# Modulation vectors: the four column tiles of the matmul array take columns of a block, and one transposition gives shift or scale

## The chip, the core and the metric

The program runs on one core of a Trainium2 chip. The metric is the device time of one execution in microseconds (us), as a median over runs. A core has TensorE for matmuls (PE, with its weight loads shown apart as PEld), VectorE (DVE), ScalarE (ACT), GpSimd (POOL) and SyncE (SP, which here mostly issues DMAs). SBUF is the on-chip memory that the engines read, PSUM the accumulator memory that TensorE writes.

## The reference

Two layers of a diffusion backbone run over 256 latent tokens and 256 context tokens of width 1024. Each layer first makes its modulation (adaLN) from two condition vectors, `c` for the latents and `c_ctx` for the context:

```python
for i in range(DEPTH):                                   # DEPTH = 2, D_MODEL = 1024
    mod_l = silu(c)     @ w_mod[i] + b_mod[i]            # 1024 -> 6144
    mod_c = silu(c_ctx) @ w_mod[i] + b_mod[i]
    sh1, sc1, g1, sh2, sc2, g2       = split(mod_l, 6)
    csh1, csc1, cg1, csh2, csc2, cg2 = split(mod_c, 6)
    zl = split_cols((layernorm0(x)     * (1 + sc1)  + sh1)  @ w_in[i])
    zc = split_cols((layernorm0(h_ctx) * (1 + csc1) + csh1) @ w_in[i])
    ...                                                  # four token mixers, merge gates, w_out
    x = layernorm(alpha * x + g1 * y_l)
    x = layernorm(alpha * x + g2 * conv_ffn(layernorm0(x) * (1 + sc2) + sh2))
    ...                                                  # the same for h_ctx with csh2, csc2, cg1, cg2
```

A modulation is thus a matrix with two rows (one for each condition) times `w_mod`, with 1024 rows and 6144 columns a layer. It is a small part of the arithmetic and a large part of the weights: 50 MB of f32 for both layers. Shift and scale are wanted with the 1024 features on the partitions (as per-partition scalars), the gates g1 and g2 as rows.

## The kernel before

**Weights.** All weights stand in one tensor of tiles `in_wt`, 128 x 1024 f32 (512 KB) each, in the order in which the program uses them. SP issues their DMAs into buffers `wraw`. For the large products a tile is split on ACT (`wH`, the value rounded to fp32r) and on DVE or POOL (`wL`, the rest), and products are summed of high and low parts (`gft`, `gtf`, `up`: input projections and the ConvFFN). A tile of `w_mod` is used as it is, in fp32, and needs no split.

**Modulation.** `w_mod` falls into 24 blocks of 512 columns (12 a layer: `nb` 0 to 11, kind `nb // 2` = shift1, scale1, gate1, shift2, scale2, gate2), each of four tiles, so 96 tiles. `mod_jobs` (from L781) makes four jobs of a block. A job waits for its tile and issues four matmuls of 128 x 32 weights (`cz`, the two conditions in 32 columns, one chunk of 128 of the 1024 rows) by 128 x 256 moving columns. They stand in the four column tiles of the array, 32 columns each, so they run side by side: column tile k takes another chunk of rows, and the result `modp`, 128 partitions x 512, holds four partial sums for each condition. Behind the fourth tile ACT copies `modp` to `modrow` (128 x 512). What follows depends on the kind:

- Shift or scale (16 blocks): four matmuls `modcp` take a 128 x 128 piece of `modrow` as the weights and the constant `sel` (128 x 2, ones at every 32nd partition) as the moving operand. That sums the four partial sums and puts the features on partitions. DVE adds bias into `modc`, which the modulation of the tokens (`modulate`, tiles `xmt`, `xmH`, `xms`, `xm`, `xmL`) reads.
- Gate (8 blocks): one matmul `modr` takes `sel` as the weights and `modrow` as the moving operand. DVE adds the bias (`modbm`), and a DMA puts the row into DRAM for later.

**Where the tiles stand.** The first 16 tiles (blocks 0, 2, 1, 3 of layer 0) are the start of the program: nothing else can go before them. Their accumulators come from the pool of the projections (`pgt`, three banks), those of all later blocks from `pq`, which has one. 52 tiles (13 blocks: nine of shift or scale, four of gates) are fill: they are put one by one between the projections of layer 0's mixers. 28 tiles (table LATE, blocks of layer 1) stand at the ends of stages: before layer 0's ConvFFN, between the layers, and before layer 1's ConvFFN.

**What sets the order.** The program is written out by a planner (`Net`, from L118). It keeps an estimated clock for every engine, adds the estimated duration of each instruction to it, and takes what could start first (`pump` L297): the next step of the weight stream (`pick` L353, `feed` L368, `splitter` L386), or one of the threads of the mixers, which carry chains of small steps (names `gd_`, `ret_`, `hg_`, `lru_`, `ro_`). An engine runs its instructions in the order that comes out. So an instruction with another shape also moves others, on all engines.

Of the kernel before, what the change touches and what calls it, by code (L numbers as in the profile page):

```python
# [9 lines left out]
F32 = mybir.dt.float32  # L10
# [4 lines left out]
ALU = mybir.AluOpType  # L15
# [102 lines left out]
class Net:  # L118
# [440 lines left out]
    def load_consts(self):  # L559
        const, I, V, A, S = self.const, self.I, self.V, self.A, self.S  # L560

        c0 = const.tile([128, 8, 2], F32, name="c0")
        S.dma_start(c0, I["cc"])
        self.sel_c = const.tile([128, 2], F32, name="sel")
        S.dma_start(self.sel_c, I["c_sel"])
        th = const.tile([128, 8, 2], F32, name="cth")
        A.activation(th, c0, AF.Tanh, scale=0.5)
        V.scalar_tensor_tensor(th, in0=th, scalar=1.0, in1=c0, op0=ALU.add, op1=ALU.mult)
        self.cz = const.tile([128, 8, 32], F32, name="cz")
        V.memset(self.cz, 0.0)  # L570
        V.tensor_scalar(self.cz[:, :, 0:2], th, 0.5, None, op0=ALU.mult)
        ck = self.ck = const.tile([128, 6, 128], F32, name="ck")
        self.ident, self.UI, self.LI, self.US, self.LS, self.perm = (ck[:, j, :] for j in range(6))
        self.par = [const.tile([128, NP], F32, name=f"par{i}") for i in range(DEPTH)]
        for i in range(DEPTH):
            S.dma_start(self.par[i], I["par"][i])
        self.msk = const.tile([128, 1664], U8, name="msk")
        self.hgm = self.msk[:, 0:1024].rearrange("p (l t) -> p l t", l=8)
        self.gdm = self.msk[:, 1024:1536].rearrange("p (l d t) -> p l d t", l=2, d=2)
        self.umask = self.msk[:, 1536:1664]  # L580
        self.ones = const.tile([128, 128], F32, name="ones")
        V.memset(self.ones, 1.0)
        self.modc = [const.tile([128, 4, 8, 2], F32, name=f"modc{i}") for i in range(DEPTH)]
        self.rowd = [self.dr.tile([2, 2, 1024], F32, name=f"rowd{i}") for i in range(DEPTH)]
# [196 lines left out]
    def mod_jobs(self, i, nb, early=False):  # L781

        mm = self.PE.matmul
        st = {}

        def mk(kk):
            def run():
                if kk == 0:
                    if early:
                        st["row"] = self.tile(self.fw, [128, 512], F32, "f_row", "modrow", 4)  # L790
                        st["ps"], st["rec"] = self.pgt([128, 512], "modp")
                    else:
                        if self.mod_th is not None:
                            self.finish(self.mod_th)
                        st["row"] = None
                        st["ps"], st["rec"] = self.tile(self.pq, [128, 512], F32, "modp", "modp", 1), []
                W, ps = self.next_tile()[0], st["ps"]
                half, kh = kk % 2, kk // 2

                for k in range(4):  # L800
                    mm(ps[32 * k:32 * k + 32, half * 256:half * 256 + 256], self.cz[:, kh * 4 + k, :], W[:, k * 256:(k + 1) * 256],
                       start=(kk == 0), stop=(kk == 3))
                if kk == 3:
                    self.evac(st["rec"], ps, evac)
                    self.mod_th = st["rec"][0]
                yield

            def evac(ps):
                row = st["row"] if early else self.ev([128, 512], "modrow")
                self.A.activation(row, ps, AF.Copy)  # L810
                kind = nb // 2
                if kind in (2, 5):
                    half, c0 = kind // 3, (nb % 2) * 512
                    yield "PE", [row], "free"
                    pr = self.pmt([128, 512], "modr")
                    mm(pr[0:2, :], self.sel_c, row, start=True, stop=True)
                    bm = self.ev([2, 512], "modbm")
                    self.S.dma_start(bm, self.I["bm"][i, nb:nb + 1, :].partition_broadcast(2))
                    yield "DVE", [bm, pr]

                    self.V.tensor_tensor(bm, bm, pr[0:2, :], op=ALU.add)
                    self.V.tensor_scalar(bm, bm, 0.5, None, op0=ALU.mult)
                    self.S.dma_start(self.rowd[i][half, :, c0:c0 + 512], bm)
                    return
                yield "PE", [row], "free"
                kind = {0: 0, 1: 1, 3: 2, 4: 3}[kind]
                pc = self.pmt([128, 4, 2], "modcp")
                for j in range(4):
                    mm(pc[:, j, :], row[:, j * 128:(j + 1) * 128], self.sel_c, start=True, stop=True)
                j0 = (nb % 2) * 4  # L830
                b0 = _P["bm"][0] + kind * 8 + j0
                self.V.scalar_tensor_tensor(self.modc[i][:, kind, j0:j0 + 4, :], in0=pc, scalar=float(kind % 2),
                                            in1=self.par[i][:, b0:b0 + 4].unsqueeze(2).broadcast_to([128, 4, 2]), op0=ALU.add, op1=ALU.add)
            j = _Job([(("w_mod", i, nb * 512 + (kk % 2) * 256, 4, 256, (kk // 2) * 4), 1024)], run)
            j.mode = "plain"
            j.early = early
            j.cost = MOD_EVERY
            return j
        return [mk(kk) for kk in range(4)]


# [1346 lines left out]
def _constants():  # L2188
    c = {}
# [18 lines left out]
    hgm[:, 0, :] = u == t  # L2208

    c["c_msk"] = np.ascontiguousarray(np.concatenate([z.reshape(128, -1).astype(np.uint8) for z in (hgm, gdm, u < t)], axis=1)).view(np.float32)  # L2210
    sel = np.zeros((128, 2), np.float32)
    for j in range(2):
        sel[j::32, j] = 1.0
    c["c_sel"] = sel
    pos = np.arange(256)
    inv = (np.float32(10000.0) ** (-np.arange(16, dtype=np.float32) / np.float32(16))).astype(np.float32)
    rope = np.zeros((128, 2, 256), np.float32)
# [30 lines left out]
def _host_arrays(a, specs):  # L2248
# [13 lines left out]
    for i in range(DEPTH):  # L2262
# [19 lines left out]
        for d in range(2):  # L2282
            for ty, nm in enumerate(("lru_w_a", "lru_w_i")):
# [3 lines left out]
    out["bm"] = a["b_mod"].reshape(DEPTH, 12, 512)  # L2287
    out.update(par=par, parf=parf, nw=nw, rows=rows, lruw=lruw)
    out.update(_constants())
    return out  # L2290


_SHAPES = dict(wt=(N_TILES, 128, 1024), x=(1, 256, 1024), ctx=(1, 256, 1024), cc=(128, 8, 2), par=(DEPTH, 128, NP),
               nw=(DEPTH, 128, 2, 128), rows=(DEPTH, 4, 1024), bm=(DEPTH, 12, 512), parf=(DEPTH, 128, 176), lruw=(DEPTH, 128, 4, 4, 128), c_f32=(128, 6, 128),
               c_msk=(128, 416), c_sel=(128, 2), c_rope=(128, 2, 256),
               c_ret=(4, 128, 2, 384))


# [22 lines left out]
```

## Time and profile before

| | |
|---|---|
| median of 3 runs | 2223.8 us (2223.27 to 2225.72) |
| profiled execution | 2219.78 us, its span 2218.0 us |
| PE busy | 2039.0 us, 92% of the span |
| DVE busy | 1495.4 us, 67% |
| ACT busy | 868.6 us, 39% |
| POOL busy | 427.3 us, 19% |
| granted clock of TensorE, mean | 0.965 of full speed |

The profile is of one execution. Its span is the time from the first to the last instruction, and 1.78 us of that execution lie around the span. A row of a timeline gives a start in us from the span's start, a duration in us, the engine, the operation with the tiles that it writes and reads, a shape, and the idle time ahead of it with what ended it. An fp32 matmul of the program leaves two records on PE, and the same for its weight load. The durations of overlapping records can't be added; what a group costs is the time from its first start to the next group's first start.

### The profile page before, as it was taken

The numbers are of one execution on the slowest core, as the hardware profiler recorded it, in microseconds if no ns is written. First come the engines' busy times: TensorE is split into PE (matmuls) and PEld (weight loads), VectorE is DVE, ScalarE is ACT, GpSimd is POOL, SyncE is SP. The second block draws the span as 40 slices with busy tenths as digits, with TensorE's granted clock in tenths as the row PEclk, the third lists the DMA queues.
The fourth block names the chain that finished last, engine by engine and source line by source line (L and its number), as shares of the span: only waits on it lengthen the run. The fifth ranks groups of instructions, "written<-read, shape, count | busy, mean of one in ns | idle before, by whom it ended". The sixth has DMA issues, their size and how long they took to land. (4 is left out here: it accounts for less than half of the span.)

```text
span 2218.0 us, 33680 instructions
## 1 busy us (share of the span) xinstructions
PE 2039.0 (92%) x13236; PEld 1749.5 (79%) x13236; DVE 1495.4 (67%) x2520; ACT 868.6 (39%) x1277; POOL 427.3 (19%) x442
## 2 busy tenths in 40 slices
PE   6999999999999999789999976998989999879997
PEld 4766777788889878678898865887978989867895
DVE  6787565445738368986646678787476566778786
ACT  4555331322222323344314434556332333326562
POOL 0163216220101001200000022273225221200000
PEclk9999999999999999889999998999999999989999
DMA  7544434424141567462223244354324422566553
GB/s 298 201 133 150 154 124 129 129 98 140 67 136 64 170 217 241 148 218 95 98 93 98 97 147 166 108 169 119 120 96 130 142 72 63 184 245 229 176 185 109
DMA packets 129679, 319.35 MB, mean 144 GB/s; under 512 B 29136, under 2 KB 51568, under 8 KB 129520
## 3 DMA queue, kind: packets, MB, share of 16 engines
q1 hardware_dynamic: 128000, 312.17, 42.7%
q0 software_dynamic: 832, 2.54, 0.4%
q8 instruction: 104, 1.70, 0.3%
q10 hardware_dynamic: 688, 2.49, 0.3%
q14 instruction: 55, 0.45, 0.1%
HBM read 294.05 MB, written 23.10 MB: 143 GB/s over the span
## 5 line engine op out<-in xcount | busy, mean ns | idle before, releaser
L85 DVE TENSOR_TENSOR wL<-wraw,wH 128x1024 fp32r<-128x1024 f32 (+2 forms) x339 | 419.4, 1242 | 172.9 <-ACT wH L85 167.6
L85 ACT ACTIVATE wH<-wraw 128x1024 fp32r<-128x1024 f32 (+1 forms) x395 | 407.9, 1036 | 233.3 <-PE gtf L85 150.7
L85 POOL TENSOR_TENSOR wL<-wraw,wH 128x1024 fp32r<-128x1024 f32 (+2 forms) x56 | 131.5, 2350 | 933.7 <-ACT wH L85 860.0
L85 PE MATMUL gft<-xmH,wH 128*128 128x512 f32 (+1 forms) x544 | 215.4, 400 | 7.4 <-DVE g_th L85 3.8
L85 PE MATMUL gft<-xmL,wH 128*128 128x512 f32 (+1 forms) x544 | 205.2, 382 | 0.0
L85 PE MATMUL gft<-xms,wH 128*128 128x256 f32 x1344 | 188.5, 292 | 8.0 <-DVE gd_yv L85 2.8
L85 PEld LDWEIGHTS gft<-xms,wH 128*128 128x128 f32 x1344 | 173.5, 197 | 15.4 <-issue 11.2
L85 DVE SCALAR_TENSOR_TENSOR ffy<-up,parf,ffy 128x255 f32<-128x255 f32 (+1 forms) x188 | 110.8, 589 | 74.7 <-ACT ffy L85 70.3
L85 PE MATMUL up<-xmL,wH 128*128 128x512 f32 (+1 forms) x400 | 144.4, 369 | 3.5 <-DVE xmL L85 3.5
L85 PE MATMUL up<-xmH,wH 128*128 128x512 f32 (+1 forms) x400 | 144.0, 368 | 0.0
L85 PEld LDWEIGHTS gft<-xmH,wH 128*128 128x128 f32 x544 | 103.1, 190 | 46.7 <-issue 17.5
L85 PE MATMUL gft<-xmH,wL 128*128 128x512 f32 (+1 forms) x544 | 133.2, 383 | 1.2 <-DVE wL L85 0.9
L85 PE MATMUL gtf<-wH,hidH 128*128 128x256 f32 (+1 forms) x352 | 114.4, 341 | 16.4 <-DVE gy L85 15.7
L85 PE MATMUL gtf<-wH,xmH 128*128 128x256 f32 (+1 forms) x384 | 109.8, 313 | 13.9 <-DVE gy L85 11.9
L85 PEld LDWEIGHTS gft<-xmL,wH 128*128 128x128 f32 x544 | 103.3, 190 | 17.4 <-issue 0.7
L85 PEld LDWEIGHTS gft<-xmH,wL 128*128 128x128 f32 x544 | 97.3, 189 | 20.9 <-DVE wL L85 1.1
L85 PE MATMUL gtf<-wH,hidL 128*128 128x256 f32 (+1 forms) x352 | 113.8, 340 | 0.0
L85 PE MATMUL gtf<-wH,xmL 128*128 128x256 f32 (+1 forms) x384 | 106.1, 303 | 0.0
L85 PE MATMUL gft<-xms,wL 128*128 128x256 f32 x672 | 99.1, 293 | 5.0 <-POOL wL L85 4.9
L85 ACT ACTIVATE ffy<-up,parf 128x256 f32<-128x256 f32 (+1 forms) x94 | 61.3, 652 | 107.4 <-PE up L85 106.8
L85 PE MATMUL up<-xms,wH 128*128 128x256 f32 x704 | 93.0, 285 | 2.0 <-ACT wH L85 1.8
L85 PE MATMUL mg_b<-brH,wH 128*128 128x256 f32 (+1 forms) x288 | 89.8, 332 | 5.2 <-ACT brH L85 3.1
(327 smaller groups left out, 4291.7 us busy)
## 6 DMA issues: line engine op xcount, KB each, us to landing
wraw<-in_wt SPq DMA_DIRECT2D x475, 512.0 KB
thd<-mg_t SPq DMA_DIRECT2D x32, 256.0 KB
mg_th<-thd SPq DMA_DIRECT2D x32, 256.0 KB
lnw<-in_rows SPq DMA_DIRECT2D x8, 512.0 KB
thd<-mg_t SPq DMA_DIRECT2D x32, 128.0 KB
xmm<-thd SPq DMA_DIRECT2D x16, 256.0 KB
brd<-ro_b SPq DMA_DIRECT2D x28, 128.0 KB
ret_tab<-in_c_ret SPq DMA_DIRECT2D x16, 192.0 KB
```

The source lines that it names most:

```text
L85: r = f(*a, **k)
```

## The change

A tile of `w_mod` now holds two chunks of 128 rows by 512 columns of a block (before: four chunks by 256 columns). A job issues eight matmuls of 128 x 32 weights by 128 moving columns: column tile j takes columns 128 j to 128 j + 127 of the block, and all eight chunks of rows are summed in the same place. `modp` is 128 x 128, with the sums complete: partition 32 j + w holds condition w for the j-th 128 columns. ACT copies 128 x 128. Shift and scale come out of one transposition, of which DVE reads two of each 32 columns. A gate takes four matmuls with two columns of the unit matrix as weights. The accumulators of the first 16 tiles are in `pq` as well, with the one buffer, and before a block begins there the planner first writes out the rest of the block before it (`finish`). The constant `sel` and its DMA are gone. The bytes and the number of the weight tiles are the same.

```diff
-        self.sel_c = const.tile([128, 2], F32, name="sel")
-        S.dma_start(self.sel_c, I["c_sel"])
...
                 if kk == 0:
-                    if early:
-                        st["row"] = self.tile(self.fw, [128, 512], F32, "f_row", "modrow", 4)
-                        st["ps"], st["rec"] = self.pgt([128, 512], "modp")
-                    else:
-                        if self.mod_th is not None:
-                            self.finish(self.mod_th)
-                        st["row"] = None
-                        st["ps"], st["rec"] = self.tile(self.pq, [128, 512], F32, "modp", "modp", 1), []
+                    if self.mod_th is not None:
+                        self.finish(self.mod_th)
+                    st["ps"], st["rec"] = self.tile(self.pq, [128, 128], F32, "modp", "modp", 1), []
                 W, ps = self.next_tile()[0], st["ps"]
-                half, kh = kk % 2, kk // 2
-
-                for k in range(4):
-                    mm(ps[32 * k:32 * k + 32, half * 256:half * 256 + 256], self.cz[:, kh * 4 + k, :], W[:, k * 256:(k + 1) * 256],
-                       start=(kk == 0), stop=(kk == 3))
+
+                for k in range(2):
+                    for j in range(4):
+                        mm(ps[32 * j:32 * j + 32, :], self.cz[:, kk * 2 + k, :], W[:, k * 512 + j * 128:k * 512 + (j + 1) * 128],
+                           start=(kk == 0 and k == 0), stop=(kk == 3 and k == 1))
...
-                row = st["row"] if early else self.ev([128, 512], "modrow")
+                row = self.tile(self.fw, [128, 128], F32, "f_row", "modrow", 4) if early else self.ev([128, 128], "modrow")
                 self.A.activation(row, ps, AF.Copy)
...
-                    pr = self.pmt([128, 512], "modr")
-                    mm(pr[0:2, :], self.sel_c, row, start=True, stop=True)
+                    pr = self.pmt([128, 4, 128], "modr")
+                    for j in range(4):
+                        mm(pr[0:2, j, :], self.ident[:, 32 * j:32 * j + 2], row, start=True, stop=True)
...
-                pc = self.pmt([128, 4, 2], "modcp")
-                for j in range(4):
-                    mm(pc[:, j, :], row[:, j * 128:(j + 1) * 128], self.sel_c, start=True, stop=True)
+                pc = self.pmt([128, 4, 32], "modcp")
+                self.PE.transpose(pc.rearrange("p j c -> p (j c)"), row, self.ident)
...
-                self.V.scalar_tensor_tensor(self.modc[i][:, kind, j0:j0 + 4, :], in0=pc, scalar=float(kind % 2),
+                self.V.scalar_tensor_tensor(self.modc[i][:, kind, j0:j0 + 4, :], in0=pc[:, :, 0:2], scalar=float(kind % 2),
...
-            j = _Job([(("w_mod", i, nb * 512 + (kk % 2) * 256, 4, 256, (kk // 2) * 4), 1024)], run)
+            j = _Job([(("w_mod", i, nb * 512, 2, 512, kk * 2), 1024)], run)
```

The planner's estimates of the new shapes move other instructions. At the start of the program, PE's order before, from tile 9 of `w_mod` to the first projection `gft` (`ck` holds the unit matrix, `xmt` are the transpositions of the normed tokens, the context's first):

```order
L85 MATMUL xmt<-ck,x_119 128x128 x8
L85 MATMUL xmt<-ck,x_121 128x128 x8
L85 MATMUL modp<-wraw_208,cz 32x256 x4
L85 MATMUL modp<-wraw_214,cz 32x256 x4
L85 MATMUL modp<-wraw_220,cz 32x256 x4
L85 MATMUL modp<-wraw_232,cz 32x256 x4
L85 MATMUL modcp<-sel,modrow 128x2 x4
```

The same place now:

```order
L85 MATMUL modp<-wraw_209,cz 32x128 x8
L85 MATMUL xmt<-ck,x_117 128x128 x8
L85 MATMUL xmt<-ck,x_119 128x128 x8
L85 MATMUL modp<-wraw_219,cz 32x128 x8
L85 MATMUL modp<-wraw_229,cz 32x128 x8
L85 MATMUL modp<-wraw_249,cz 32x128 x8
L85 MATMUL modcp<-ck,modrow 128x128
```

One tile of weights went ahead of the context's transpositions; behind these rows both orders have four more tiles, their `modcp`, the latents' transpositions, one tile and the first `gft`. On ACT at the same place, before (`xmH` is the modulated input, `ea` and `lbe` are exponentials for the mixers of layer 1, `wH` the splits of the first projection's tiles):

```order
L85 ACTIVATE xmH<-xmt,modc_109 128x256 x8
L85 ACTIVATE modrow<-modp 128x512
L85 ACT_TABLE_LOAD
L85 ACTIVATE ea_387<-par_103 128x8
L85 ACTIVATE lbe<-lbe 128x16
L85 ACTIVATE modrow<-modp 128x512
L85 ACTIVATE xmH<-xmt,modc_109 128x256 x8
L85 ACTIVATE wH<-wraw 128x1024 x2
```

ACT now:

```order
L85 ACTIVATE xmH<-xmt,modc_107 128x256 x8
L85 ACTIVATE modrow<-modp 128x128 x2
L85 ACTIVATE xmH<-xmt,modc_107 128x256 x8
L85 ACT_TABLE_LOAD
L85 ACTIVATE ea_496<-par_101 128x8
L85 ACTIVATE lbe<-lbe 128x16
L85 ACTIVATE wH<-wraw 128x1024 x2
```

The table load, `ea` and `lbe` moved from the front of the latents' `xmH` to behind it, right ahead of the first `wH`. What `lbe` reads comes from DVE, where the small steps that lead to it moved in the same way. DVE now, from the last `modc` on (before, the steps `sp_lw` to `lbe` stood ahead of the four pairs of `xm` and `xmL`, between the third and the fourth `modc`):

```order
L85 SCALAR_TENSOR_TENSOR modc_107<-modcp,par_100 128x8 x2
L85 TENSOR_SCALAR xm_451<-xmt,modc_107 128x256 x2
L85 TENSOR_TENSOR xmL<-xm_451,xmH 128x2x256
L85 TENSOR_SCALAR xm_462<-xmt,modc_107 128x256 x2
L85 TENSOR_TENSOR xmL<-xm_462,xmH 128x2x256
L85 TENSOR_SCALAR xm_473<-xmt,modc_107 128x256 x2
L85 TENSOR_TENSOR xmL<-xm_473,xmH 128x2x256
L85 TENSOR_SCALAR xm_484<-xmt,modc_107 128x256 x2
L85 TENSOR_TENSOR xmL<-xm_484,xmH 128x2x256
L85 TENSOR_TENSOR sp_lw_311<-sp_lw_311,sp_q_309 128x8
```

In layer 1's mixers PE's order changes too. Before, the chain of a `gdn` scan (steps `gd_`, each of which waits for DVE or ACT to finish the one before) had pieces of a projection between its steps. One place, before:

```order
L85 MATMUL gft<-xms_11767,wL 128x256 x4
L85 MATMUL gd_Tt<-ck,gd_T 128x128 x8
L85 MATMUL gft<-xms_11767,wL 128x256 x4
L85 MATMUL gft<-xms_11347,wH 128x256
L85 MATMUL gft<-xms_11767,wH 128x256
```

The same chain now, from the same step on (`ret_` and `ro_` are steps of another mixer):

```order
L85 MATMUL gd_Tt<-ck,gd_T 128x128 x8
L85 MATMUL gtf<-wH,xms_12075 128x256 x8
L85 MATMUL gtf<-wL,xms_12075 128x256 x4
L85 MATMUL gd_Y<-gd_T,gd_B 128x128 x4
L85 MATMUL gd_X<-gd_Ys,gd_T 128x2x32 x8
L85 MATMUL gd_XT<-gd_T,gd_Ys 128x128 x4
L85 MATMUL gd_Y<-gd_T,gd_B 128x128 x4
L85 MATMUL gd_XT<-gd_T,gd_Ys 128x128 x4
L85 MATMUL ro_t<-ck,ret_ob 128x128 x2
L85 MATMUL ret_s<-ret_r 128x256 x2
L85 MATMUL gd_pw<-gd_T,gd_ek 64x128 x8
L85 MATMUL ret_s<-ret_r 128x256 x2
```

From `gd_Y` to the last `gd_dS` the chain has no projection between its steps any more; the projection stands behind it.

## Rows read from the trace of the kernel before

**Rows 1.** The page, busy time of each engine, share of the span, instructions.
```profile
PE 2039.0 (92%) x13236; PEld 1749.5 (79%) x13236; DVE 1495.4 (67%) x2520; ACT 868.6 (39%) x1277; POOL 427.3 (19%) x442
```

**Rows 2.** Stretches: length, busy PE, PEld, DVE, ACT, POOL, clock, DMA share, GB/s.
```profile
24.00:32.00 8.00, 7.06 (x39) 6.11 (x43) 3.71 (x16) 5.97 (x14) 0.00 (x0) 1.00 1.03 403
...
45.00:535.00 490.00, 470.76 (x3037) 364.49 (x3037) 303.89 (x581) 189.86 (x296) 154.09 (x184) 0.99 0.44 142
1690.00:1768.00 78.00, 72.23 (x587) 69.12 (x586) 49.95 (x82) 29.08 (x50) 42.53 (x62) 0.98 0.47 147
```

**Rows 3.** Timeline of PE (start, duration, operation, shape), one tile in the fill.
```profile
65.39 0.64 PE L85 MATMUL modp<-wraw,cz 128*32 128x256 f32 x8
65.96 0.39 PE L85 MATMUL gtf<-wH,xmH 128*128 128x256 f32 x1
```

**Rows 4.** Timeline of PE, four tiles behind each other, and what follows.
```profile
35.35 1.94 PE L85 MATMUL modp<-wraw,cz 128*32 128x256 f32 x32
38.00 1.05 PE L85 MATMUL modcp<-sel,modrow 128*128 128x2 f32 x8 [0.72 <-ACT modrow L85]
38.92 1.94 PE L85 MATMUL xmt<-ck,x 128*128 128x128 f32 x16
...
44.34 0.39 PE L85 MATMUL gft<-xmH,wH 128*128 128x256 f32 x1 [2.91 <-ACT wH L85]
```

**Rows 5.** Timeline of PE, a group with two column tiles of 64 and 128 moving columns.
```profile
211.74 1.09 PE L85 MATMUL gd_pw<-gd_T,gd_ek 128*64 128x128 f32 x16
212.76 0.66 PE L85 MATMUL gd_pq<-ck,gd_qe 128*128 128x128 f32 x4
```

**Rows 6.** Groups by tile: count, duration in ns (least, median, most), first and last start.
```profile
L85 PEld LDWEIGHTS modp<-wraw,cz x768: 106/109/178, 8.8 to 2006.1; 128*32 128x32 f32 x192
...
L85 ACT ACTIVATE modrow<-modp x24: 577/597/602, 22.1 to 2008.3; 128x512 f32<-128x512 f32 x24
...
L85 PEld LDWEIGHTS gd_pw<-gd_T,gd_ek x128: 132/137/137, 211.7 to 1781.7; 128*64 128x64 f32 x128
```

**Rows 7.** Timeline of PE, a `modcp` in the fill, and a single transposition elsewhere.
```profile
391.45 0.95 PE L85 MATMUL modcp<-sel,modrow 128*128 128x2 f32 x8
392.26 0.48 PE L85 MATMUL gft<-xmH,wH 128*128 128x512 f32 x1
...
1626.79 0.38 PE L85 MATMUL gd_t<-ck,gd_yqk 128*128 128x128 f32 x2
1626.93 0.84 PE L85 MATMUL gft<-xms,wL 128*128 128x256 f32 x5
```

**Rows 8.** Timelines of ACT and DVE at the start.
```profile
37.19 0.21 ACT L85 ACTIVATE lbe<-lbe 128x16 f32<-128x16 f32 x1 [1.35 <-DVE lbe L85]
...
43.20 2.04 ACT L85 ACTIVATE wH<-wraw 128x1024 fp32r<-128x1024 f32 x2
...
36.10 0.16 DVE L85 TENSOR_TENSOR sp_lw<-sp_lw,sp_q 128x8 f32<-128x8 f32 x1
...
40.65 1.00 DVE L85 TENSOR_SCALAR xm<-xmt,modc 128x256 f32<-128x256 f32 x2 [1.15 <-ACT xmH L85]
...
42.29 0.99 DVE L85 TENSOR_SCALAR xm<-xmt,modc 128x256 f32<-128x256 f32 x2
```

**Rows 9.** Timeline of PE, the two waits behind the first projection tiles.
```profile
53.03 0.39 PE L85 MATMUL gft<-xmH,wH 128*128 128x256 f32 x1 [0.78 <-ACT wH L85]
...
56.08 1.10 PE L85 MATMUL gft<-xmH,wL 128*128 128x256 f32 x7 [0.88 <-DVE wL L85]
```

**Rows 10.** Timeline of PE between the layers and in layer 1's `gdn` chain.
```profile
1370.85 1.01 PE L85 MATMUL modr<-modrow,sel 128*2 128x512 f32 x1 [12.03 <-ACT modrow L85]
...
1745.11 1.05 PE L85 MATMUL gd_Y<-gd_T,gd_B 128*128 128x128 f32 x8
1745.91 1.19 PE L85 MATMUL gft<-xms,wH 128*128 128x256 f32 x8
...
1764.70 0.66 PE L85 MATMUL gd_dS<-gd_u,gd_kt 128*64 128x128 f32 x8
```

More of the change, by code (lines that the diff above doesn't have):

```diff
@@ L819, in evac @@
                     yield "DVE", [bm, pr]
-                    self.V.tensor_tensor(bm, bm, pr[0:2, :], op=ALU.add)
+                    self.V.tensor_tensor(bm, bm, pr[0:2].rearrange("p j c -> p (j c)"), op=ALU.add)
                     self.V.tensor_scalar(bm, bm, 0.5, None, op0=ALU.mult)
@@ L2210, in _constants @@
     c["c_msk"] = np.ascontiguousarray(np.concatenate([z.reshape(128, -1).astype(np.uint8) for z in (hgm, gdm, u < t)], axis=1)).view(np.float32)
[L2211 to L2214, printed above, removed]
     pos = np.arange(256)
@@ L2294 @@
                nw=(DEPTH, 128, 2, 128), rows=(DEPTH, 4, 1024), bm=(DEPTH, 12, 512), parf=(DEPTH, 128, 176), lruw=(DEPTH, 128, 4, 4, 128), c_f32=(128, 6, 128),
-               c_msk=(128, 416), c_sel=(128, 2), c_rope=(128, 2, 256),
+               c_msk=(128, 416), c_rope=(128, 2, 256),
                c_ret=(4, 128, 2, 384))
```

## The prediction

> **What bounds the kernel now.** First the engines' busy times: PE is busy 92% of the span and no other engine over 67% [rows 1], so PE's order of work is nearly the path of the whole program, and what matters is where PE's time is really paid. The stretches tell that [rows 2]. From 45 to 535 us, where 52 of the 96 modulation tiles lie as fill, PE is busy 470.76 of 490 us at a clock of 0.99, while the DMA engines are busy 0.44 of the time: there a microsecond taken out of PE's row comes off the end. Before that, up to 32 us, the DMA share is 1.03 at 403 GB/s: the first 16 tiles are waited for, and PE's time under them is free. Third, the waits at the ends of stages and in layer 1, read from the timeline.
>
> **The change part by part, the matmuls.** One tile in the fill takes 0.57 us, from its start at 65.39 to the next group's at 65.96 [rows 3]. Four tiles in a row take 1.94 us of busy time [rows 4], one alone 0.64, so three more cost 1.30, or 0.433 a tile: two rounds of the four column tiles, 0.217 for 256 columns. The rest, 0.57 − 0.433 = 0.137, is paid once for a group. Now a tile has four rounds of 128 columns. What such a round costs is seen in `gd_pw`, which has two column tiles of 64 and the same 128 columns: 1.02 us to the next group [rows 5], so (1.02 − 0.137)/8 = 0.110 a round, with its weight loads in it, whose records last 0.132 to 0.137 [rows 6]. So a tile becomes 0.137 + 4 × 0.110 = 0.577, or 0.01 more. There are twice as many loads and matmuls to issue, so I take 0.02, nearer to `gd_pw` than to the other end. That end is a round no shorter than one of its loads, 0.137: 0.137 × 5 = 0.685, 0.115 more. Below, nothing is to be gained, since the same columns stream. 52 tiles: +1.0 us (0 to +6.0).
>
> **The rule against it.** In `gd_pw` every load uses all 128 rows, and a new round still starts each 0.110 us [rows 5]. The Trainium skill, page "TensorE: Matmul & The Clock Gate", section "Part 3: Packing small matmuls — row/col tiling", says that a weight load overlaps running matmuls only where its row group differs. By that rule the loads here could not hide, and the two more rounds of a tile would each show one. The trace of `gd_pw` speaks against it, and the rule's outcome stands below as a rival.
>
> **The transposition.** A `modcp` in the fill holds PE from 391.45 to 392.26, 0.81 us, since each of its four matmuls loads 128 x 128 weights for two columns. A single transposition elsewhere takes from 1626.79 to 1626.93, 0.14 us [rows 7]. That is 0.67 less a block; the cautious end counts the transposition at its whole record time, 0.38, so 0.43 less. Nine such blocks lie in the fill: −6.0 us (−3.9 to −6.0). This is the main gain.
>
> **Gates, copies, DVE.** A gate's four matmuls stream the same 512 columns as the one before; four of them in the fill, at nothing (±0.3). ACT's copy shrinks from 0.58 us [rows 6] toward the 0.21 of its smallest steps [rows 8]; ACT is busy 39% of the span [rows 1], so in the fill this is hidden and would cost nothing were it longer. DVE's `modc` reads as many numbers as before. One small DMA at the start goes. The weights are the same bytes. The first 16 tiles now share one accumulator bank, so a block's first tile waits for the copy of the block before; at 403 GB/s [rows 2] a tile of 512 KB lands every 1.3 us, which covers a copy of under 0.58.
>
> **The start.** Before, the last early `modcp` begins at 38.00, the latents' `xmt` at 38.92, DVE's first `xm` at 40.65 and the first `gft` at 44.34, behind 2.91 us of idle PE [rows 4, 8]. Tiles 13 to 16 had landed by 35.35, where PE took them without a wait [rows 4]; PE now reaches them earlier, and the chain behind them loses most of a `modcp` and of a copy. DVE is free for the latents at 36.1, where its small steps began [rows 8]; I put the first `xm` at 36.2 (37.9 at the latest estimate). But ACT's `wH` now stands behind `lbe`, and `lbe` behind DVE's four pairs of `xm` and `xmL`. A pair takes 42.29 − 40.65 = 1.64, four 6.6; the small steps from `sp_lw` to `lbe` 37.19 − 36.10 = 1.09; `lbe` itself 0.21 [rows 8]. So `lbe` ends at 36.2 + 6.6 + 1.1 + 0.2 = 44.1, the first `wH` (half of 2.04) at 45.1, and `gft` starts at 45.2, 0.9 later than before. In return the two waits behind it, 0.78 and 0.88 for `wH` and `wL` [rows 9], should go, since ACT and DVE have nothing but splits left by then: −1.7. Together −0.7 us (−1.7 if `gft` keeps its place, +2.6 if `xm` starts at 37.9 and the two waits stay).
>
> **The ends of stages.** The 28 late tiles stand beside layer norms and DMAs. A copy is the last thing that PE waits for at one place, `modr` at 1370.85 behind 12.03 us of idle [rows 10]; it is some 0.3 shorter. The three `modcp` there stand before normed tokens that come later anyway. Taken −0.3 (−2.3 if those three paid in full, to 0).
>
> **Layer 1's order.** Before, the `gdn` chain ran from 1745.11 to 1764.70, 19.6 us, and ten pieces of `gft` like that at 1745.91 (8 records, 1.19 busy, about 1.05 in place) stood between its steps [rows 10], 10.5 us of cover. Now steps of another mixer stand there and the projection comes behind. If these cover half, 5 us of waiting show; but the projection is not lost, and it can fill what was idle around: 78.00 − 72.23 = 5.8 us from 1690 to 1768 [rows 2]. I take 0 (−5.8 if all that idle goes, +10.5 if no cover is left and nothing else is filled).
>
> **Sum.** 1.0 − 6.0 + 0 − 0.7 − 0.3 + 0 = −6.0 us. The profiled execution took 2219.8, so 2213.8 by its measure. The median of the runs is 4.0 above that execution, so 2217.8.
>
> **The rivals.** *The order gives it back.* The start goes to +2.6 instead of −0.7 and layer 1 shows 3 us: −6.0 + 3.3 + 3 = +0.3, 2224.1. For it: PE's idle of the start is set by ACT and DVE, which now carry more ahead of the first `wH`. Against: two waits there are due to fall. *The order also helps*: −5.8 in layer 1 gives 2212. *The order costs*: all cover lost in layer 1, −6.0 + 10.5 = +4.5, 2228.3. *The gain does not arrive*: the stage ends in 45 to 535 us are set by chains of DVE and ACT steps, PE's saved time becomes idle, 2223.8; PE's 96% there speak against it. *The loads are not hidden*, the rival on the other side: every further round of a tile shows a load of 0.109 us [rows 6]. Two rounds more make +0.22 a tile; on the 80 tiles outside the DMA-bound start +17.6, and with the −7.0 of all else +10.6: 2234.4. The sign turns where 80 tiles cost 7.0, at a round of (0.433 + 0.0875)/4 = 0.130 us, just under the record of a load in `gd_pw`; it is slower by more than 0.2% from 0.144 on. The round of 0.110 speaks against it, the four loads in place of two for it.
>
> **How the numbers follow.** 0.2% of 2223.8, 4.4 us, is about what a measurement of this kernel can tell from no change. Chances: my forecast 0.48 (its own range 2212 to 2219), the order helps too 0.07; the order gives it back 0.26 and the gain does not arrive 0.07, both the same time; loads not hidden 0.07, the order costs 0.05. So faster 0.55, same 0.33, slower 0.12. The range from 2210 to 2229 takes in all but the loads, and the outer ends of the bounds at the start and in layer 1.
>
> **What the profile will show.** `modp` with 1536 records, a tile in the fill at 0.57 to 0.60 us to the next group (at 0.65 or more the loads show); `modcp` with 32 records and about 0.14 us to the next group; PE's busy time from 45 to 535 us lower for the same work, and the end of layer 0's mixers 4 to 6 us earlier; the first `gft` near 45.2 with no wait of over 0.5 us in the next 12 us; from 1690 on, PE's idle near 6 us in the same piece of work. I am wrong if the first `gft` comes after 46, if the `gd_` steps of layer 1 wait for over 5 us more than before, or if a round takes over 0.13 us.

## The result: 0.6% slower, and the profile after

| | before | changed |
|---|---|---|
| median of 4 runs | 2223.5 us (2221.8 to 2225.7) | 2238.8 us (2232.6 to 2243.1) |
| ratio, 95% interval | | 1.0062 (1.0044 to 1.0080) |
| the same on another chip | 2224.7 us (26 runs) | 2236.5 us (7 runs), ratio 1.0054 (1.0035 to 1.0073) |

The forecast was 2217.8 us, 2210 to 2229. By the two ratios the change costs 12 to 14 us. Two traced executions are compared below: that of before (2219.8 us) lies below its four runs, that of the changed kernel (2243.1 us) is the slowest of its four, so their spans differ by 23.3 us, more than the medians. A second trace of the changed kernel (2233.1 us) is named where it differs. The first lines of the page (span; busy time; granted clock of TensorE by slices) answer to [rows 1]:

```profile
span 2241.3 us, 35029 instructions
...
PE 2037.2 (91%) x13940; PEld 1769.8 (79%) x13940; DVE 1492.4 (67%) x2528; ACT 861.3 (38%) x1277; POOL 411.1 (18%) x434
...
PEclk9998999999999999989999998999999899988998
```

PE's busy time is hardly lower, 2037.2 in place of 2039.0 us, and the span is 23.3 us longer, so PE's idle time grew by 25 us (17.6 in the second trace). That is one part of the loss. The other is hidden in the busy time: E1 below does the same operations in the order of before with 2029.0 us of it. Some of the changed kernel's matmuls run at half clock and so stay busy for longer, as the places below show.

**The operations themselves came out as worked out.** The groups of the tiles, and PE's timeline at one tile, one `modcp` and one gate (start, duration, operation):

```profile
L85 PEld LDWEIGHTS modp<-wraw,cz x1536: 106/110/178, 7.5 to 2029.8; 128*32 128x32 f32 x192
L85 PE MATMUL modp<-wraw,cz x1536: 269/273/423, 7.5 to 2030.0; 128*32 128x128 f32 x192
L85 ACT ACTIVATE modrow<-modp x24: 259/277/311, 17.0 to 2031.4; 128x128 f32<-128x128 f32 x24
```

```profile
58.91 0.64 PE L85 MATMUL modp<-wraw,cz 128*32 128x128 f32 x16
59.48 0.39 PE L85 MATMUL gft<-xmH,wH 128*128 128x256 f32 x1
...
60.15 1.04 PE L85 MATMUL modr<-modrow,ck 128*2 128x128 f32 x8
61.11 0.39 PE L85 MATMUL gft<-xmH,wH 128*128 128x256 f32 x1
...
145.56 0.27 PE L85 MATMUL modcp<-ck,modrow 128*128 128x128 f32 x1
145.76 0.64 PE L85 MATMUL modp<-wraw,cz 128*32 128x128 f32 x16
```

A tile takes 0.57 us to the next group, as before [rows 3]; with sixteen records in place of eight nothing of the loads shows. A `modcp` takes 0.20 here (0.81 before [rows 7]), a gate 0.96 (0.95 before).

**Where the time went.** Starts in the traces of the kernels, in us (the kernels E1 to E12 are those of the next section; "fill" is the last of the 52 fill tiles, "L1" the first late tile between the layers, "F1" the first late tile ahead of layer 1's ConvFFN):

| kernel | first gft | fill | L1 | F1 | F1 − L1 | span |
|---|---|---|---|---|---|---|
| before | 44.3 | 529.5 | 1356.5 | 1986.4 | 629.9 | 2218.0 |
| changed | 46.1 | 546.0 | 1372.8 | 2009.2 | 636.4 | 2241.3 |
| changed, second trace | 44.9 | 541.1 | 1364.6 | 1998.0 | 633.4 | 2231.3 |
| E1, new sums, order of before | 43.0 | 530.9 | 1358.3 | 1987.9 | 629.6 | 2219.9 |
| E2, old sums, order of after | 48.4 | 548.8 | 1374.1 | 2010.0 | 635.9 | 2242.0 |
| E3, chain held | 45.5 | 529.2 | 1355.3 | 1992.0 | 636.8 | 2223.9 |
| E4, lbe first | 41.2 | 525.7 | 1350.9 | 1987.3 | 636.4 | 2219.4 |
| E5, both | 41.5 | 520.8 | 1348.5 | 1968.1 | 619.7 | 2199.9 |
| E7, chain's DMAs on GpSimd, new sums | 42.3 | 531.5 | 1356.5 | 1992.8 | 636.3 | 2225.4 |
| E8, the same, kernel before | 44.0 | 541.7 | 1369.6 | 2012.5 | 642.8 | 2245.0 |
| E9, old sums, order of E5 | 42.5 | 521.8 | 1347.7 | 1972.0 | 624.2 | 2206.9 |
| E10, work in two waits | 45.5 | 542.1 | 1368.2 | 1998.5 | 630.3 | 2230.7 |
| E11, work in six waits | 45.5 | 541.0 | 1367.5 | 1992.9 | 625.4 | 2224.9 |
| E12, E5 and work in its waits | 41.2 | 517.9 | 1344.3 | 1963.4 | 619.1 | 2195.6 |

The changed kernel loses 16.5 us by the end of the fill, nothing from there to layer 1, and 6.5 us in layer 1's mixers. In its second trace these are 11.6, a gain of 3.5, and 3.5, so single places are known to a few us only. Three places stand out.

*One: the chain of layer 0's first gdn scan.* The timelines of PE, DVE, GpSimd and SP of the changed kernel, at PE's step `gd_Tt`:

```profile
178.84 0.39 PE L85 MATMUL gft<-xmL,wH 128*128 128x512 f32 x1
...
192.94 0.48 PE L85 MATMUL gd_Tt<-ck,gd_T 128*128 128x128 f32 x1 [13.71 <-DVE gd_T L85]
...
191.97 0.91 DVE L85 COPY gd_T<-gd_Z 32x128 f32<-32x128 f32 x4 [12.77 <-DMA gd_Z<-blk]
...
185.24 0.15 POOL L85 MEMSET gd_z<- 64x32 f32 x1
...
185.42 0.46 SPq L85 DMA_DIRECT2D blk<-gd_z  x1
...
188.49 0.93 SPq L85 DMA_DIRECT2D gd_Z<-blk  x2
```

The same place before:

```profile
183.40 0.15 POOL L85 MEMSET gd_z<- 64x32 f32 x1
...
192.24 0.91 DVE L85 COPY gd_T<-gd_Z 32x128 f32<-32x128 f32 x4
...
194.84 0.39 PE L85 MATMUL gft<-xmL,wH 128*128 128x512 f32 x1
195.06 0.38 PE L85 MATMUL gd_Tt<-ck,gd_T 128*128 128x128 f32 x2
```

GpSimd inverts blocks of the gdn system step by step (`gd_z`), SP carries them to DRAM and back in another layout (`blk`, `gd_Z`), DVE and ACT copy them into `gd_T`, and PE turns them (`gd_Tt`). The chain on GpSimd ends at 185.39 in place of 183.55, only 1.8 us later. But PE comes to `gd_Tt` at 179.2 in place of 195.1, because the planner put that step ahead of some pieces of the projection that stood in front of it before. PE then stands still for 13.71 us, with work ready behind the waiting step. In the second trace of the changed kernel the wait is 10.95 us. Before, DVE's first copies ended at 193.15, so PE came 1.9 us after them; that was all the slack that can be read there.

*Two: the start.* PE and ACT of the changed kernel:

```profile
37.35 0.64 PE L85 MATMUL modp<-wraw,cz 128*32 128x128 f32 x16
46.06 0.58 PE L85 MATMUL gft<-xmH,wH 128*128 128x256 f32 x1 [8.06 <-ACT wH L85]
46.44 0.41 PE L85 MATMUL gft<-xmL,wH 128*128 128x256 f32 x1
46.65 0.41 PE L85 MATMUL gft<-xmH,wH 128*128 128x256 f32 x1
...
44.84 0.22 ACT L85 ACTIVATE lbe<-lbe 128x16 f32<-128x16 f32 x1 [3.42 <-DVE lbe L85]
44.96 1.99 ACT L85 ACTIVATE wH<-wraw 128x1024 fp32r<-128x1024 f32 x2
```

PE is done with the early tiles 3.4 us sooner than before, and ACT's `wH`, behind `lbe`, lets it start 1.7 us later: 8.06 us of idle time in place of 2.91 [rows 4]. And the matmuls behind it start 0.21 us from each other; before it was 0.12. They ran at half clock. In the second trace the wait is 8.05 us and the first `gft` at 44.9. (The words ahead of the prediction call the second group of `xmt` and `xmH` the latents' one. It is the second half of the features, for both kinds of tokens; the sums on it don't change.)

*Three: layer 1's clock.* PE's idle time from L1 to F1 is the same in both kernels, 70.8 us, yet the stretch is 6.5 us longer (68.6 us idle and 3.5 us longer in the second trace). The first of the places is the step `gd_t` (changed, then before):

```profile
1429.94 0.66 PE L85 MATMUL gd_t<-ck,gd_yv 128*128 128x128 f32 x4 [4.32 <-DVE gd_yv L85]
...
1431.65 1.49 PE L85 MATMUL gd_t<-ck,gd_qk 128*128 128x128 f32 x6
```

```profile
1412.44 0.44 PE L85 MATMUL gd_t<-ck,gd_yv 128*128 128x128 f32 x2 [2.18 <-DVE gd_yv L85]
1412.71 0.82 PE L85 MATMUL gd_t<-ck,gd_qk 128*128 128x128 f32 x6
```

The six records take 1.49 us in place of 0.82. The stretches behind the three waits (first `gft`, `gd_Tt`, `gd_t`), and the gdn chain whose pieces of `gft` had gone (length; busy PE, PEld, DVE, ACT, POOL; clock; DMA share; GB/s), changed first, then the places of the three waits before:

```profile
46.00:52.00 6.00, 5.94 (x36) 5.70 (x40) 2.88 (x6) 1.37 (x4) 0.00 (x0) 0.51 0.26 90
...
192.90:198.90 6.00, 4.62 (x18) 3.84 (x19) 0.00 (x0) 2.42 (x6) 0.00 (x0) 0.52 0.53 210
...
1429.00:1441.00 12.00, 10.49 (x52) 8.21 (x53) 6.23 (x14) 6.82 (x13) 3.27 (x3) 0.72 0.16 45
...
1752.80:1772.80 20.00, 14.85 (x85) 11.60 (x85) 10.37 (x37) 3.34 (x7) 0.00 (x0) 0.73 0.38 124
```

```profile
44.00:50.00 6.00, 5.36 (x44) 4.61 (x45) 5.93 (x8) 1.71 (x3) 2.39 (x1) 1.00 0.34 116
...
195.00:201.00 6.00, 5.17 (x34) 4.02 (x33) 5.86 (x9) 5.36 (x9) 0.00 (x0) 1.00 0.28 93
...
1412.00:1424.00 12.00, 11.56 (x87) 10.21 (x88) 9.68 (x23) 7.67 (x17) 2.91 (x2) 1.00 0.27 88
```

### The profile page after: what moved, and what is told of

Same layout as the page of the kernel before. It is cut to its first block, busy times and chain, and to the rows that moved or that the text cites. A ratio compares the mean times of both kernels' runs of the same rounds, so it can differ in the third digit from the quotient of the medians.

```text
span 2241.3 us, 35029 instructions
## 1 busy us (share of the span) xinstructions
PE 2037.2 (91%) x13940; PEld 1769.8 (79%) x13940; DVE 1492.4 (67%) x2528; ACT 861.3 (38%) x1277; POOL 411.1 (18%) x434
## 5 line engine op out<-in xcount | busy, mean ns | idle before, releaser
L85 DVE TENSOR_TENSOR wL<-wraw,wH 128x1024 fp32r<-128x1024 f32 (+1 forms) x345 | 424.3, 1236 | 168.3 <-ACT wH L85 168.0
L85 POOL TENSOR_TENSOR wL<-wraw,wH 128x1024 fp32r<-128x1024 f32 (+2 forms) x50 | 116.3, 2328 | 949.1 <-ACT wH L85 900.8
L85 PE MATMUL gtf<-wH,xmH 128*128 128x256 f32 (+1 forms) x384 | 109.2, 311 | 13.6 <-DVE gy L85 11.9
```

The source lines that it names most:

```text
L85: r = f(*a, **k)
```

## The experiments

Ratios are to the kernel before on the same chip, with 95% intervals. The planner keeps the same code in all of them; what is edited is the numbers that it is given, the point at which it writes out one thread (E4), or an instruction outside of its sight.

**E1 and E2: order and arithmetic apart.** Theory A: the planner's new order costs the time, and the operations gain what was worked out. Theory B: the new operations cost the time in a way that the trace hides. E1 does the new sums, and the planner is told the old durations; every instruction but those of the modulation then stands where it stood before. E2 is the reverse: old sums, new durations, the order of the changed kernel. The accumulators go with the order: E1 has the three banks of before for the first 16 tiles, E2 the one buffer of the changed kernel.

```diff
# E1, on the changed kernel (planner: d = self.force where it is set)
+                self.force = (max(4 * 256 / 2400.0, 0.2) + 0.01) * 0.28 / 2   # modp as before
...
+                self.force = 0.1 + 512 / 1200.0                               # modrow as before
                 self.A.activation(row, ps, AF.Copy)
...
+                self.force = 0.84                                             # modcp as before
                 self.PE.transpose(pc.rearrange("p j c -> p (j c)"), row, self.ident)
```

> The new arithmetic in exactly the order of before: the planner is given the durations of the old shapes for modp, modrow, modcp and modr, and the first 16 tiles use the three accumulator banks of before. Theory A (the order costs the time, the operations themselves gain what was worked out): 6 us under before, 2215 to 2220, PE idle as in before, no wait of over 2 us at gd_Tt near 195, first gft at 42 to 44.5. Theory B (the new operations themselves cost the time, through loads or hand-overs that the trace hides): close to the changed kernel, 2233 to 2243.

> The old arithmetic in exactly the order of the changed kernel: the planner is given the durations of the new shapes. Theory A: as late as the changed kernel or later by the gain of the operations, 2236 to 2250, with PE idle for over 10 us ahead of gd_Tt near 180 and the first gft near 46 to 49. Theory B: close to before, 2220 to 2228.

E1: 2221.7 us against 2225.7, ratio 0.9980 (0.9969 to 0.9992). E2: 2243.7 us, ratio 1.0078 (1.0057 to 1.0099), with 11.16 us of idle ahead of `gd_Tt` and the same 8.06 us ahead of the first `gft`. Theory A holds: the order alone (with its one buffer) makes the old kernel 0.8% slower, and the operations alone make it 0.2% faster, 1.8 to 6.9 us where 6.0 had been worked out and 2215 to 2220 us expected. In the order of after the old sums are 3 to 6 us slower than the new ones by medians against the kernel before; there the intervals overlap. E1's first `gft` is at 43.0, its longest wait at `gd_Tt` 1.30 us. That the one buffer costs the time is ruled out by E3, E4 and E5, which keep it.

E1's trace also shows where a part of the operations' gain goes: from the first `gft` to the end of the fill PE is busy 2.0 us less than before and idle 4.8 us more, and the fill ends no earlier (530.9, 529.5 before, in traces that lie 2 us apart). From 186 us on PE waits for weights, which it did not before:

```profile
188.37 0.65 PE L85 MATMUL modp<-wraw,cz 128*32 128x128 f32 x16 [2.10 <-DMA wraw<-in_wt]
...
190.79 0.79 PE L85 MATMUL gft<-xmH,wH 128*128 128x512 f32 x1 [1.78 <-ACT wH L85]
```

SP issues the weights' DMAs and, in the same queue, `blk`, which waited 13.6 us for GpSimd's chain in E1. So what PE saves ahead of that point it may wait for there; E7 tests that.

**E3: the chain held.** One number in the planner: the end of GpSimd's chain in layer 0's first scan is taken 12 us later.

```diff
             E.memset(z[:, 0::33], 1.0)
+            if (i, g) == (0, 0):
+                self.rdy[z.tensor.name]["POOL"] += HOLD      # 12.0
             yield "SP", [z]
```

> The changed kernel, with one number in the planner: the result of GpSimd's chain of block inverses in layer 0's first gdn scan is taken as ready 12 us later, so that PE's order has gd_Tt behind more of the projection. If the 13.71 us of idle PE ahead of gd_Tt are the main loss: 11 to 15 us under the changed kernel, 2223 to 2229, start unchanged (first gft near 46). Rival (the wait only moves to another step of the chain or of layer 1): 2233 to 2243.

2222.4 us, ratio 0.9992 (0.9979 to 1.0004), 14 to 16 us under the changed kernel. PE reaches `gd_Tt` at 200.2 and does not wait there; the start (45.5) and layer 1's stretch (636.8) are as in the changed kernel. So the wait at `gd_Tt`, with the half clock behind it, was the main loss. The one number moves some hundreds of instructions of the fill with it, but neither the start nor layer 1's stretch gets better.

**E4: lbe first.** The small steps that end in `lbe` are written out ahead of the second half of the modulated input.

```diff
+                if first and d == 4:
+                    self.finish(self.ct)          # ct: the thread of these steps
             ps = self.pmt([128, 2, 2, 128], "xmt")
...
-        ct = self.spawn(self.derive())
+        ct = self.ct = self.spawn(self.derive())
```

> The changed kernel, with the small steps that end in lbe written out ahead of the second half of xmH, as in before. If the start's loss is ACT's wH behind lbe: first gft at 40.5 to 42.5 in place of 46.1, at full clock from the first matmul on, 5 to 8 us less. In the order that comes out, gd_Tt also stands behind 9 us more of the projection, so if that wait is the main loss another 11 to 14 us go: 2216 to 2223. If only the start matters: 2230 to 2234. If neither: 2238.

2221.2 us, ratio 0.9978 (0.9968 to 0.9988). The first `gft` is at 41.2, 4.9 us sooner, but still at half clock, behind a wait of 4.26 us: the clock part of the expectation was a miss. `gd_Tt`, which now has more of the projection in front, waits 1.0 us. One moved step at the start thus undid most of two of the three losses, the second through the order that came with it. Layer 1's stretch stayed at 636.4.

**E7 and E8: the chain's DMAs on another queue.** The DMAs `blk` and `gd_Z` are issued by GpSimd, in E1 (E7) and in the kernel before (E8); all engines keep their order.

```diff
+    def on_pool(self, out, in_):
+        self.nc.gpsimd.dma_start(out, in_)
+        self.account("SP", "dma_start", (out, in_), {})
...
-            self.S.dma_start(self.blk[1].rearrange("p i j -> p (i j)"), z)
+            self.on_pool(self.blk[1].rearrange("p i j -> p (i j)"), z)
...
-                self.S.dma_start(Z[:, :, w, :], self.diag(1, seg, w))
+                self.on_pool(Z[:, :, w, :], self.diag(1, seg, w))
```

> The new arithmetic in the order of before, with the DMAs that carry the block inverses out and back (blk, gd_Z) issued by GpSimd in place of SP. If PE's saved time ahead of 186 us is lost because the weight tiles stand in SP's queue behind a DMA that waits for GpSimd's chain: the idle of 2.1 us for wraw and 1.8 us for wH at 186 to 191 goes, 2 to 4 us under the same kernel with SP, 2217 to 2220. Rival (PE then waits for gd_Tt by as much, since the chain itself ends no earlier): the same 2221 to 2223, with a longer wait at gd_Tt near 193.

> The kernel before, old arithmetic and old order, with the same DMAs issued by GpSimd. If SP's queue costs only what is early: no change within 2 us, 2223 to 2227, since there PE reached the same place as the weights did (0.8 us of idle at most from 180 to 200). If the queue cost every gdn scan of the kernel something: 3 to 6 us faster.

E7: 2229.0 us, ratio 1.0017 (1.0000 to 1.0034). E8: 2233.4 us, ratio 1.0036 (1.0021 to 1.0050). Both expectations missed. In E7 the two waits for weights near 190 are gone, as the theory of the queue says, and two others stand in their place, 1.35 and 2.28 us at `gd_Tt`:

```profile
188.62 0.66 PE L85 MATMUL gd_Tt<-ck,gd_T 128*128 128x128 f32 x4 [1.35 <-DVE gd_T L85]
191.55 0.66 PE L85 MATMUL gd_Tt<-ck,gd_T 128*128 128x128 f32 x4 [2.28 <-ACT gd_T L85]
```

So SP's queue was one of two things that end at nearly the same time; the chain is the other. E7's loss against E1 lies in layer 1, whose stretch is 636.3 us in place of 629.6. There the wait at `gd_Tt` grew from 8.13 us (E1) to 10.16 (E7), and from 7.04 (before) to 11.19 (E8). From the end of GpSimd's chain to `gd_Tt` it is 6.4 us where SP issues the DMAs and 9.5 where GpSimd does, in both pairs; GpSimd itself stands still for 2.6 us until `blk` has landed. In layer 0's first scan it is the other way: 8.7 us to the first copy of `gd_T` with SP, 6.7 and 7.2 with GpSimd. E8's trace is of the slowest of its 13 executions, so only what E7 shows as well is read from it; why E8 loses more is open.

**E5 and E9: both edits, and whose gain it is.** E5 is the changed kernel with the edits of E3 and E4. E9 has E5's order and the old sums.

> Both edits of the planner's numbers in one kernel: lbe ahead of the second half of xmH, and the chain of block inverses taken as ready 12 us later. If the start's loss and the wait at gd_Tt are separate and layer 1's loss is a third: close to the kernel with lbe first, since that one had lost the wait at gd_Tt too, 2217 to 2222; under 2215 only if layer 1's order comes out without its 4 us wait at gd_t near 1405.

> The changed kernel itself, beside the runs of this call, for comparisons on one chip and for a second trace. If the wait at gd_Tt is a fixed property of the order: again 12 to 15 us of idle PE ahead of it, and 2236 to 2242 where the kernel before has 2224 to 2226. If it was an accident of the one traced execution: under 5 us there.

> The old arithmetic in exactly the order of the kernel with both edits (lbe first, chain held by 12 us), which took 2201.7. If that kernel's 23 us come mostly from the order that it happens to get and the new operations give their 4 to 6 us on top, as in the order of before: 2205 to 2209. If the new operations are what makes that order good: 2215 or more.

E5: 2201.7 us against 2224.7, ratio 0.9903 (0.9880 to 0.9927), the fastest kernel here. The changed kernel measured beside it: 2236.5, ratio 1.0054. E9: 2212.7 us, ratio 0.9946 (0.9926 to 0.9966). The expectation for E5 was a miss to the good side: layer 1's stretch came out at 619.7 us, 10 shorter than before, by an order that nobody asked for, and with a wait of 3.71 us at `gd_t` still in it. By E9, which lies between the two outcomes that its expectation gave, that order gives some 12 us and the new sums another 9 to 11 (each ratio is known to 4 or 5 us either way). Whether the sums give more here than in the order of before is open, as the intervals overlap; why this order suits layer 1 was not shown.

**E10, E11, E12: work in the waits.** Is it the idle time that lowers the clock? E10 adds matmuls to the changed kernel, whose results are overwritten: 16 of 256 columns ahead of the first `gft` and 4 of 512 ahead of layer 1's `gd_t`. E11 adds 4 of 256 columns ahead of each of four read-outs `ro_t` near the gdn chain. Nothing moves, PE only has more to do. E12 does it in E5, with 8 in place of 16 ahead of the first `gft`.

```diff
+    def warm(self, ps, n):
+        m = self.ck.rearrange("p a b -> p (a b)")[:, 0:ps.shape[-1]]
+        for _ in range(n):
+            self.nc.tensor.matmul(ps, self.ident, m, start=True, stop=True)
...
             ps, rec = self.pgt([128, 512], "gft")
+            if not self.warmed:
+                self.warmed = True
+                self.warm(ps[:, 0:256], 16)
             yield from self.gemm_ft(ps[:, :n], HL, *self.xf(tsl.start, tsl.stop), 8)
```

> The changed kernel with added matmuls whose results are overwritten: 16 of 256 columns ahead of the first gft, inside the 8.06 us wait for wH, and 4 of 512 columns ahead of layer 1's gd_t, inside its 4.3 us wait for gd_yv. Nothing else moves. If the idle time itself makes TensorE's granted clock fall behind it: the first gft then runs at full clock (about 0.12 us from one start to the next in place of 0.21) and so does the stretch of 12 us behind gd_t; 4 to 8 us under the changed kernel, 2228 to 2233. If the clock falls for another reason: the same low clock in both places and no gain, 2236 or more.

> The changed kernel with the added matmuls of the run before it (ahead of the first gft and of layer 1's gd_t), and four more of 256 columns (1.7 us) ahead of each of the four read-outs ro_t of layer 1's retention, which wait 1.6 to 2.7 us for ret_ob. If layer 1's second stretch of low clock (0.69 to 0.73 in 20 us around 1750 to 1770) comes from the gdn chain standing there without other work: the clock there at 0.85 or more, layer 1's stretch 2 to 5 us shorter than with the first two places alone, in all 2229 to 2232. If not: the same low clock there, and 0 to 2 us longer, since 1.7 us are added where 1.6 us were free: 2234 to 2236.

> The kernel with both edits of the planner's numbers (2201.7 before) and added matmuls in its waits: 8 of 256 columns (3.4 us) ahead of the first gft, inside a wait of 4.26 us, and the places of layer 1 as in the runs before. If low clock behind waits is what is left to gain there: first gft at full clock and 2 to 4 us less there, another 2 to 6 us in layer 1, so 2193 to 2199. If that order has no such stretch worth the added work: 2201 to 2204.

E10's timeline and stretches at the two places:

```profile
45.49 0.38 PE L85 MATMUL gft<-xmH,wH 128*128 128x256 f32 x1 [1.20 <-ACT wH L85]
45.71 0.28 PE L85 MATMUL gft<-xmL,wH 128*128 128x256 f32 x1
45.83 0.28 PE L85 MATMUL gft<-xmH,wH 128*128 128x256 f32 x1
```

```profile
1748.20:1768.20 20.00, 17.21 (x103) 14.86 (x100) 11.87 (x35) 5.42 (x9) 0.00 (x0) 0.68 0.49 159
1423.00:1435.00 12.00, 10.30 (x67) 7.90 (x67) 8.86 (x19) 7.42 (x14) 3.23 (x3) 1.00 0.14 44
46.00:52.00 6.00, 6.00 (x62) 5.67 (x61) 4.03 (x7) 2.19 (x4) 0.00 (x0) 1.00 0.49 139
```

At both places the clock is 1.00 where it had been 0.51 and 0.72; at the gdn chain, untouched in E10, it is still 0.68. E11 there:

```profile
1747.50:1767.50 20.00, 18.74 (x147) 16.34 (x146) 13.74 (x38) 9.63 (x19) 0.00 (x0) 1.00 0.66 224
```

With work in six waits the time follows. E10: 2233.9 us, ratio 1.0042 (1.0027 to 1.0058), just outside of what had been expected, and by itself not clear of the changed kernel, as the intervals overlap. E11: 2225.3 us, ratio 1.0009 (0.9998 to 1.0020), better than the 2229 to 2232 us that had been expected, and clear: a kernel with some 17 us more work on PE is 10 to 13 us faster than the changed one. The gain is in layer 1, which takes 625.4 us where the traces of the changed kernel have 636.4 and 633.4. The first wait gives nothing that can be seen at the end of the fill, 542.1 and 541.0 us in E10 and E11 and 546.0 and 541.1 in the changed kernel: behind it stands the wait at `gd_Tt`, still 12.48 and 10.85 us. E12: 2204.0 us, ratio 0.9914 (0.9896 to 0.9933), no better than E5: its first `gft` runs at full clock too, but filling the same places gains nothing in that order.

## Why the prediction was wrong

**What was right.** The matmuls (0.57 us a tile where 0.577 had been worked out), the transposition (0.20 and less in place of 0.81), the gates at nothing, the ends of stages at nothing to speak of. E1 is that sum without the new order: 1.8 to 6.9 us faster. The rival of the loads has fallen: twice as many of them hide whole. The Trainium skill, "TensorE: Matmul & The Clock Gate", section "Part 3: Packing small matmuls — row/col tiling", says that a weight load overlaps running matmuls only where its row group differs. This trace does not agree: all loads of a tile use the same rows, and sixteen records of 0.110 us lie within its 0.57 us.

Two readings were off, with little effect. The row that gave 0.14 us for a single transposition [rows 7] holds two, as a transposition leaves one record and not two; the profile has 16 records of `modcp`, and not 32. And the start's terms, 0.9 and −1.7, make −0.8 in place of −0.7.

**The step that failed: the sum had no term for layer 0's order.** The order was weighed at the start and in layer 1, and nowhere else; that `gd_Tt` of layer 0 had moved ahead of some 9 us of the projection was in the order, and it was costed at nothing, because no wait of before stood there. But a step that waits for nothing is a step whose slack the trace can tell. Before, GpSimd's chain ended at 183.55, the way through DRAM and DVE's first copies took until 193.15, and PE reached `gd_Tt` at 195.06: 1.9 us to spare. An order that brings PE there 16 us sooner must wait. It did, 11 to 14 us, with a clock of 0.52 over the 6 us behind the wait, and E3 gives back 14 to 16 us.

**The start was right for the first `gft`, and had no term for the clock behind it.** `lbe` did move ahead of `wH` and it did set the first `gft`, where 45.2 had been put: at 46.1 in this trace, and at 44.9 in the second and 45.5 in E3, which have the same start. The sign of being wrong, a first `gft` after 46, thus came by chance of one execution. The two waits behind it, worth 1.7, did go. What the working left out is that PE's idle time ahead of `gft` grew from 2.91 to 8.06 us, and that PE then ran at half clock for 6 us, which by an estimate from these 6 us costs some 3. So −0.7 became +1.7 at the first `gft` and +3.5 at the modulation tile behind it (51.47 in place of 47.97).

**Layer 1's term was right in idle time and wrong in time.** 0 had been taken, with −5.8 to +10.5; the idle time changed by 0.0 (−2.2 in the second trace), and the stretch by +6.5 (+3.5), in PE's busy time and not in its waits. The clock at 1430 and 1753 is lower than before, and work alone brings that stretch from 636.4 and 633.4 to 630.3 (E10) and 625.4 (E11).

**The chances.** The cases in which order eats the gain had 0.31 together, and only 0.05 of it went to a loss above 0.2%. They were priced at single places. An order that comes out of estimated clocks moves hundreds of instructions; the five orders in which the new sums were measured (E1, the changed kernel, E3, E4, E5) lie between 2201.7 and 2238.8 us, which is wide against a gain of 6. More than half of the 1% by which E5 is faster than the kernel before comes with the old sums too (E9): that order is luck, as the loss of the changed kernel's order is bad luck.

## What to carry to other kernels

Where a planner writes the order from its own estimates, measure a change of an operation's cost with the order pinned (here: the planner told the old durations), and only then with the order free; the two effects can have opposite signs. Before predicting, list every step in the new order that PE reaches sooner than before, and hold against each the end of the chain that it waits for, also where the old trace shows no wait. Idle time of TensorE had a second price here, the clock behind it: useless work in six waits of 1.6 to 8 us made the changed kernel 10 to 13 us faster, though in E5's order the same filling gained nothing.

## What the runs showed of the hardware

The granted clock was at its lower level (0.51 in a stretch of 6 us, that is 1.2 in place of 2.4 GHz) behind 8.06 us (the changed kernel) and behind 4.26 us (E4) of idle TensorE time at the first `gft`. It stayed at the upper one there behind 2.91 us (before) and, with work put into the wait, behind 1.20 (E10). The wait ahead of it does not tell all: in E1 PE stood idle for 2.12 and again, at the first `gft`, for 1.81 us, and the clock was 0.50 from 44 to 47 us, 1 us into the projection. In the gdn chain of layer 1 the clock was 0.68 (E10) and 0.73 (the changed kernel) over 20 us of short steps, and 1.00 with 7 us of useless matmuls around that chain (E11).

The chain's round trip through DRAM (256 KB out, two pieces of 64 KB back) depends on who issues it, and not everywhere in the same sense. In layer 1's first scan it took 6.4 us from the end of GpSimd's chain to `gd_Tt` when SP issued it and 9.5 when GpSimd did (before and E1 against E7 and E8). In layer 0's first scan it took 8.7 us to the first copy with SP and 6.7 and 7.2 with GpSimd.
